# Normalised activations in tiles of 528 floats instead of 516

## The chip, the core and the metric

The kernel runs on one core of a Trainium2 chip. Its time is the device time of one execution, in microseconds (us). A profile is one execution recorded by the hardware profiler: which instruction ran on which engine, when, and what it waited for. The engines are TensorE (PE, with its weight loads shown apart as PEld), VectorE (DVE), ScalarE (ACT), GpSimd (POOL) and SyncE (SP); transfers run on 16 DMA engines. SBUF is the on-chip memory: 128 partitions, in each of which a tile takes the same bytes. "Alignment" in this text is the address of a tile within its partition, modulo 64.

## What is computed

One step of a two-layer backbone with 128 context and 128 latent tokens and a width of 2048. Per layer: a modulated RMSNorm, a mixer (attention and convolution in the first, a state-space model and grouped attention in the second), a modulated RMSNorm and an MLP with 8192 hidden features. Nearly all of the arithmetic is in the linears:

```python
for l in range(2):
    h = modulate(x, norm_g[l, 0], shift1, scale1)
    x = x + gate1 * mixer(h)                   # @ w_in, ..., @ w_out
    h = modulate(x, norm_g[l, 1], shift2, scale2)
    a = relu(h @ mlp_w1[l])
    x = x + gate2 * ((a * a) @ mlp_w2[l])
y = rms_norm(x, final_norm)
```

shift, scale and gate come from `silu(cond) @ ada_w[l] + bias`.

## The kernel before

Both token groups lie side by side as 256 columns, features on the partitions. A linear takes 128 outputs at a time: the weights come as pieces of 128x1024 floats (8 blocks of 128x128), by DMA into one of 8 `raw` tiles. Every float32 operand is split into a high half in a reduced format (F32R) and a low half, the rest. ScalarE casts the high half of a weight piece to `wh`, VectorE subtracts it to get `wl` (4 tiles each). Of activations the two halves lie in one tile: columns 0:256 high, 256:512 low. `block` (L453) then issues three matmuls for one block of weights and one tile of activations, all into the same PSUM tile `lin`: wh times high, wh times low, wl times high. `part` (L460) does so for the 8 blocks of a piece.

Tiles of activations come from two pools. The pool "hl" has 24 slots in rotation, of 516 floats each; it holds the normalised activations, the mixers' outputs and half or more of the MLP's hidden features. The pool "hid" holds the other hidden features in tiles of 512 floats: 8 in the first layer, 24 in the second. `put` (L543) fills a tile of either; both bear the name `hl` in the profile, so that hid tiles are told apart by the place in the program alone: in the w2 linears of `mlp` (L1685), tiles 0 to 7 of the 16 of a quarter of the hidden features are hid tiles and 8 to 15 hl tiles, but in the second quarter of the second layer all 16 are hid tiles. In `unnormed_tile` (L751) an hl tile holds 258 columns of each half (256 of the tokens and 2 of the shift), which is where 516 comes from; the first linears after a norm read them 258 wide, from columns 0:258 and 258:516.

A first pass, thrown away, keeps a clock for each engine and so finds the order in which the strands of the program take turns; the second builds the program in that order. Sizes of tiles in bytes play no part in it.

The pools lie one behind the other in SBUF: const (constants, among them `pk`, 866 floats loaded from one packed input, `ones`, `eps` and `pick2`), then x, "hl", raw, wh, wl, work, and the pools of a stage such as "hid". A tile's place is rounded up to 32 bytes. In the built program of before an hl tile takes 2064 bytes and 2080 of space, the first begins on a multiple of 64 bytes, and so do x, all raw, wh and wl tiles and all hid tiles. hl slots with an even number thus begin on a multiple of 64 bytes, those with an odd one 32 bytes past it. `eps` (L313) is the bias of the square root in `rstd_rows` (L659); `pick2` (L319) is a pair of 128x32 matrices with a one in column 0 or 1 and else zeros, with which `ada_vector` (L615) sums over the partitions on TensorE.

Of the kernel before, what the change touches and what calls it, by code (L numbers as in the profile page):

```python
# [19 lines left out]
EPS = 1e-6  # L20
# [28 lines left out]
class Engine:  # L49
    """An engine whose instructions are also charged to the program's clocks."""  # L50
# [27 lines left out]
class Line:  # L78
    """A strand of the program: a generator that says what its next instructions wait for."""
# [4 lines left out]
    def on_pe(self):  # L84
        """Whether its next instructions are for TensorE."""
        return callable(self.wait) and getattr(self.wait, "pe", False)
# [25 lines left out]
class Kern:  # L112
# [20 lines left out]
    # The program is many strands. A first run, that is thrown away, keeps a clock for each engine and always goes  # L133
    # on with a strand whose operands are there by then; the second run builds the program in that order, with
    # the weights loaded and split ahead of their use.
# [59 lines left out]
    def at(self, *aps):  # L195
        """When the tiles' contents are there."""
        return max([0] + [NEVER if v.tensor.name in self.held else self.at_.get(v.tensor.name, 0) for v in aps])

    def hold(self, t):
        """Not all of t is written yet."""  # L200
        self.held[t.tensor.name] = True
# [10 lines left out]
    def bulk(self, lead):  # L212
        """For work that is not urgent: the engines have come up to `lead` behind the clock of TensorE."""
        return lambda: max(self.clock["vector"], self.clock["scalar"]) + lead
# [58 lines left out]
    def get(self, *tags, on=None):  # L273
        """Waits for free slots (and for tiles), and takes them."""
        def ok():
            for t in set(tags):
                if self.live.get(t, 0) + tags.count(t) > self.cap[t]:
                    return False
            return self.when(on) + (MARGIN if "ps" in tags else 0)
        ok.pe = "ps" in tags  # L280
        yield ok
        for t in tags:
            self.live[t] = self.live.get(t, 0) + 1
# [10 lines left out]
    def setup(self):  # L294
        nc = self.nc
        self.const = self.pool("const", 1)
        self.xp = self.pool("xres", 1)
        self.hlp = self.pool("hl", 24)
        self.rawp = self.pool("raw", RAW)
        self.whp = self.pool("wh", SPLIT + 1)  # L300
        self.wlp = self.pool("wl", SPLIT + 1)
        self.work = self.pool("work", 2)
        self.ps = self.pool("ps", 1, PSUM)
        self.dram = self.pool("dram", 1, DRAM)
        pk = self.const.tile([128, _width(PACK)], F32, name="pk")
        nc.gpsimd.dma_start(pk, self.i["pack"])
        self.pk = {k: pk[:, a:b] for k, (a, b) in PACK.items()}
        self.x = self.xp.tile([128, KT, 256], F32, name="x")
        for q in range(2):
            nc.sync.dma_start(self.x[:, 8 * q:8 * q + 8], self.i["xT"][:, 8 * q:8 * q + 8])  # L310
        self.ones = self.const.tile([128, 128], F32, name="ones")
        nc.vector.memset(self.ones, 1.0)
        self.eps = self.const.tile([128, 1], F32, name="eps")  # L313
        nc.vector.memset(self.eps, EPS)
        self.ident = self.pk["ident"]
        self.condp = self.const.tile([128, KT, 32], F32, name="condp")
        nc.vector.memset(self.condp, 0.0)
        nc.scalar.activation(self.condp[:, :, 0:2], self.pk["cond"].rearrange("p (k c) -> p k c", c=2), AF.Silu)
        self.pick2 = self.const.tile([128, 2, 32], F32, name="pick2")  # L319
        nc.vector.memset(self.pick2, 0.0)  # L320
        for c in range(2):
            nc.vector.memset(self.pick2[:, c, c:c + 1], 1.0)
        self.mod, self.A, self.set_up = {}, {}, True
# [6 lines left out]
    def source(self, spec):  # L330
        """The columns of a piece, side by side."""
# [38 lines left out]
    def pump(self, upto=0):  # L370
        """Loads ahead, as far as there is room, and splits what has come (and the pieces before `upto` in any
        case)."""
# [24 lines left out]
    def slot(self, key, bufs, back=0):  # L397
        """When the slot of the next tile (or one after it) is free."""
# [4 lines left out]
    def peek(self, n, split=False):  # L403
        """When the next n raw tiles are there."""
# [5 lines left out]
    def take(self, split, *spec):  # L410
        """The next piece that has been loaded: its halves, or itself."""
# [32 lines left out]
    def there(self, X, a, b, weights=True):  # L444
        """For a wait: the tiles X[a:b], and the weights that come next."""
# [14 lines left out]
    def part(self, ps, src, X, a, b, first, last, w=None, **kw):  # L460
        """ps (+)= weight blocks a to b of a tile times X[a:b]."""
# [20 lines left out]
    def staged(self, srcs, X, width, groups, done, release=None):  # L482
        """Linears in groups: first all on the half of X that is there first."""
        n = 0
        for g in groups:
            # the first weights come before the banks are free
# [15 lines left out]
    def pairs(self, srcs, X, tags, done, cuts, between=None):  # L502
        """Linears side by side, two to a bank (of the given tags): first all on the part of X that is there first.
        done(n, ps, release) takes the tiles; between() is issued after the first part."""
# [16 lines left out]
        for i, (a, b) in enumerate(cuts):  # L521
            last = i == len(cuts) - 1
            # at the end one of each bank first: its copy out holds the bank
            for n in list(range(0, len(out), 2)) + list(range(1, len(out), 2)) if last else range(len(out)):
                ps, r = out[n]
                # the start of the first tile of a bank clears all of it
# [6 lines left out]
    def out_proj(self, src, X, done, held, between=None):  # L533
        """The tiles of an output projection, whose second half of X is there first."""
# [8 lines left out]
    def put(self, X, k, src, pool=None, slot=False):  # L543
        """X[k] = the halves of src."""
# [4 lines left out]
        t = (pool or self.hlp).tile([128, 512 if pool else 516], F32R, name="hl", tag="hl")  # L549
# [7 lines left out]
    def copied(self, dst, ps, note=None, release=None):  # L557
        """dst = ps, a linear's tile."""
# [10 lines left out]
    def ada(self, *pieces):  # L569
        """Two pieces (l, i, a, b) of the modulation: blocks a to b of vector i."""  # L570
# [44 lines left out]
    def ada_vector(self, n, pool):  # L615
        """Pieces of the modulation on VectorE, when it has time; TensorE only sums over the partitions."""
        nc = self.nc
        self.vnext = 0.0
        for piece in [(l, i, a, a + 8) for l, i in VECTOR[n] for a in (0, 8)]:
# [14 lines left out]
            for c in range(2):  # L634
                for b in range(4):
                    nc.tensor.matmul(ps[32 * b:32 * b + 32, 0:256], self.pick2[:, c], acc[:, c, 256 * b:256 * b + 256],
# [4 lines left out]
    def background(self):  # L641
        """The modulation in the order of its use: first parts of shift and scale, then theirs second."""
# [7 lines left out]
    def cuts(self, l, j):  # L650
        """The parts in which a modulated norm comes."""
        return FIRST if (l, j) == (0, 0) else ((0, 8), (8, 16))

    def mods(self, *keys):
        """For a wait: pieces of the modulation."""
        return lambda: self.at(*[self.mod[k] for k in keys]) if all(k in self.mod for k in keys) else False

# [1 line left out]
    def rstd_rows(self, sums, n, width, tag):  # L659
        """rstd of the sums in sums[:, :n] (token on the partition)."""  # L660
# [12 lines left out]
    def rstd_bcast(self, acc, width):  # L673
        """acc [128, 256]: squares summed over tiles; the rstd of each token on all partitions."""
# [20 lines left out]
    def sq_start(self, *norm):  # L695
        """The next norm's sum begins, and what doesn't wait for it."""
# [25 lines left out]
    def scales(self, l, j, a, b):  # L722
        """The factor of the modulated norm, with its gain."""
# [18 lines left out]
    # The first linears of a modulated norm don't wait for the sum over all of x: W (rstd A x + B) is  # L742
    # rstd (W A x) + W B, and B comes along as two more columns.
# [7 lines left out]
    def unnormed_tile(self, k, A, B, U):  # L751
# [8 lines left out]
        t = self.hlp.tile([128, 516], F32R, name="hl", tag="hl")  # L760
# [8 lines left out]
    def enter(self, l, j, srcs, groups, done):  # L769
        """The modulated norm of x; done(n, v, release) takes the first linears."""  # L770
# [36 lines left out]
    def residual(self, k, ps, l, i, summed, release=None, final=False):  # L807
        """x += gate * ps; the squares of the new x go to the next norm's sum if it has begun."""
# [17 lines left out]
    def softmax_parts(self, ps_list, scales, pool, tag, ebufs=2):  # L826
        """exp of the scaled scores (each a [128, 384] bank: prompt | sample) and the sums, per part."""
# [24 lines left out]
    def rope(self, out, src, rot, cos, sin, n, pool, tag, **kw):  # L852
        """out = src * cos + rot * sin for [128, n, 128] views."""
# [116 lines left out]
    def conv(self, gates, cins, cv, csum, mp, m2, mix):  # L970
# [21 lines left out]
        # layer norm of the convolution, silu  # L992
# [45 lines left out]
    def norm_heads(self, heads, ssq, ats, sub, m2, mix, hds):  # L1038
        """rms norm of the heads."""
# [206 lines left out]
    def gqa_scales(self, g, qss, qn, rqs, m2):  # L1246
        """The scale of each token's scores: rstd of the query, over sqrt(dim)."""
# [62 lines left out]
    def cmul(self, out_r, out_i, ar, ai, br, bi, tmp, neg_i=False):  # L1310
        """out = a * b, complex; tmp gives two scratch views of out's shape."""
# [13 lines left out]
    def s5_powers(self, kk, q1, z):  # L1325
# [4 lines left out]
        with ExitStack() as st:  # L1330
# [16 lines left out]
            # reduced angle: th - 2 pi n, with the product split so that it is exact  # L1347
# [33 lines left out]
            # k = (abar - 1) / a  # L1381
# [16 lines left out]
            # orders of powers: q1 for the chunk's state (7 - s | s), z for its output (i | 8 - i)  # L1398
# [111 lines left out]
    def s5(self, uts, mp, m2, fin, yhl):  # L1510
        """Two halves of the channels; the second one's states are prepared while the first one's are scanned."""
# [6 lines left out]
    def s5_states(self, qh, uts, mp, m2, out):  # L1518
        nc = self.nc
        u4 = range(4 * qh, 4 * qh + 4)  # L1520
        # u by (position in the chunk, channel) on the partition
# [29 lines left out]
        # states that each chunk adds  # L1551
# [38 lines left out]
    def s5_outputs(self, qh, u2, hs, mp, m2, fin, yhl):  # L1590
        nc = self.nc
        tt = nc.gpsimd.tensor_tensor
        # recurrence over the chunks (the backward half runs from the last)
# [22 lines left out]
        # outputs  # L1616
# [155 lines left out]
    def fill(self, most, goal, parts):  # L1772
        """How far the modulation pieces may run (in steps), and how far they have to within that many parts."""
# [47 lines left out]
def _channels():  # L1821
    """Order of the S5 channels: tile (qh, g4), partition (q', n)."""
# [101 lines left out]
```

## Time and profile before

| | |
|---|---|
| times of three runs, us | 2418.14, 2422.73, 2423.43 |
| median, us | 2422.73 |
| span of the profiled execution, us | 2417.9 |
| busy: PE, PEld, DVE, ACT, POOL | 96%, 88%, 70%, 48%, 7% |
| granted TensorE clock | 90% or more in 37 of the 40 slices |
| mean traffic of the memory | 260 GB/s |

Busy time of an engine is the time in which it ran instructions; matmuls overlap each other, so the mean duration of one is longer than the interval at which they start, and intervals are read from counts in a window or from starts in the timeline. The chain of waits goes back from the last instruction to whatever released it, and so on. [...]

### The profile page before, as it was taken

How to read it: one execution, taken by the hardware profiler on the slowest of the kernel's cores; microseconds unless marked ns; L12 is line 12 of the kernel's file. 1: busy time of each engine (PE TensorE's matmuls, PEld its weight loads, DVE VectorE, ACT ScalarE, POOL GpSimd, SP SyncE). 2: the span in 40 equal slices, each digit the busy share in tenths (PEclk: the TensorE clock that was granted, in tenths of full speed). 3: DMA queues.
4: the chain of work that ended last, by engine and by line, in shares of the span. 5: the costliest groups of instructions: out<-in, count | busy, mean ns of one | idle time of the engine just before them, and what ended most of it. 6: DMA issues, size and time to landing. Idle time of an engine off the chain costs nothing.

```text
span 2417.9 us, 49512 instructions
## 1 busy us (share of the span) xinstructions
PE 2331.7 (96%) x20152; PEld 2134.6 (88%) x20152; DVE 1696.8 (70%) x2957; ACT 1154.1 (48%) x1894; POOL 173.5 (7%) x293
## 2 busy tenths in 40 slices
PE   6999999999999999999999978999999999999997
PEld 1788887888999999999999857799999999999997
DVE  1489985677889898887666434566998855555555
ACT  2364457465444434434455644555744333443453
POOL 0000000000111011101000236000000000000000
PEclk9999999999999999999999988999999999999998
DMA  9979987879678898879877877765587855555552
GB/s 384 339 261 325 320 312 255 293 269 317 204 265 301 300 316 299 311 263 333 281 231 249 295 281 265 270 226 181 187 295 268 273 192 193 182 191 190 184 186 94
DMA packets 179638, 627.64 MB, mean 260 GB/s; under 512 B 21377, under 2 KB 21393, under 8 KB 179153
## 3 DMA queue, kind: packets, MB, share of 16 engines
q1 hardware_dynamic: 169920, 595.67, 71.1%
q0 software_dynamic: 9488, 28.81, 3.9%
q8 instruction: 158, 2.59, 0.4%
q14 instruction: 72, 0.58, 0.1%
HBM read 602.17 MB, written 26.41 MB: 260 GB/s over the span
## 4 chain that ended last, share of the span: by engine, by line
PE 85%; DVE 3%; DMA 3%; ACT 3%; POOL 3%; issue 1%; DVEq 0%; SPq 0%; ACTq 0%; POOLq 0%
PE lin L60 76%; PE ada L60 5%; POOL rt L60 2%; DVE wl L60 1%; DMA raw<-in_ada_w 1%; POOL hs L60 1%; ACT wh L60 1%; PE m1T L60 1%; DMA raw<-m3d 1%; ACT hs L60 0%; PE ps L60 0%; DMA raw<-in_ew_in 0%; PE po L60 0%; ACT L60 0%; DMA raw<-in_w 0%
## 5 line engine op out<-in xcount | busy, mean ns | idle before, releaser
L60 PE MATMUL lin<-hl,wh 128*128 128x256 f32 (+1 forms) x11200 | 2009.6, 282 | 7.2 <-ACT wh L60 7.0
L60 PEld LDWEIGHTS lin<-hl,wh 128*128 128x128 f32 x11200 | 1715.2, 189 | 98.4 <-issue 57.4
L60 PE MATMUL lin<-hl,wl 128*128 128x256 f32 (+1 forms) x5600 | 1569.9, 280 | 12.1 <-DVE wl L60 12.1
L60 PEld LDWEIGHTS lin<-hl,wl 128*128 128x128 f32 x5600 | 1058.2, 189 | 14.9 <-DVE wl L60 14.9
L60 DVE TENSOR_TENSOR wl<-raw,wh 128x1024 fp32r<-128x1024 f32 (+1 forms) x716 | 857.2, 1206 | 278.5 <-ACT wh L60 276.8
L60 ACT CAST wh<-raw 128x1024 fp32r<-128x1024 f32 (+1 forms) x716 | 738.6, 1035 | 520.0 <-PE lin L60 273.7
L60 PE MATMUL ada<-raw,condp 128*32 128x512 f32 (+1 forms) x1408 | 186.0, 572 | 19.5 <-DMA raw<-in_ada_w 19.3
L60 DVE SCALAR_TENSOR_TENSOR x<-lin,mod,x 128x128 f32<-128x128 f32 x320 | 97.1, 345 | 102.8 <-PE lin L60 102.6
L60 DVE SCALAR_TENSOR_TENSOR va<-raw,condp,va 128x1024 f32<-128x1024 f32 x120 | 148.4, 1277 | 0.0
L60 ACT ACTIVATE ms<-lin 128x256 f32<-128x256 f32 x114 | 43.8, 384 | 155.6 <-PE lin L60 155.6
L60 ACT CAST hl<-mq 128x256 fp32r<-128x256 f32 x128 | 51.8, 406 | 96.2 <-DVE mq L60 96.2
L60 DVE SCALAR_TENSOR_TENSOR cv<-cin,pke,cv 128x256 f32<-128x256 f32 x232 | 96.5, 476 | 0.0
L60 PEld LDWEIGHTS ada<-raw,condp 128*32 128x32 f32 x1408 | 32.8, 109 | 72.0 <-DMA raw<-in_ada_w 30.5
L60 DVE SCALAR_TENSOR_TENSOR mq<-lin,ms 128x256 f32<-128x256 f32 x114 | 47.9, 420 | 61.5 <-ACT ms L60 61.3
L60 ACT ACTIVATE sq<-x 128x256 f32<-128x256 f32 x75 | 31.0, 417 | 119.1 <-DVE x L60 117.1
L60 DVE TENSOR_TENSOR hl<-mq,hl 128x256 fp32r<-128x256 f32 x128 | 53.6, 421 | 28.3 <-ACT hl L60 28.1
L60 POOL TENSOR_TENSOR x<-x,rb 128x512 f32<-128x512 f32 (+1 forms) x2 | 4.2, 2133 | 916.6 <-ACT rb L60 916.6
L60 DVE TENSOR_TENSOR acc<-acc,sq 128x256 f32<-128x256 f32 x75 | 31.8, 424 | 32.2 <-ACT sq L60 30.4
L60 DVE TENSOR_TENSOR hl<-h,hl 128x256 fp32r<-128x256 f32 (+1 forms) x112 | 45.4, 420 | 9.1 <-ACT hl L60 8.7
L60 ACT CAST hl<-h 128x256 fp32r<-128x256 f32 (+1 forms) x112 | 42.8, 402 | 12.2 <-DVE h L60 11.5
L60 POOL DMA_DIRECT2D m3d<-m x32 | 21.6, 678 | 348.3 <-DVE m L60 347.1
L60 DVE TENSOR_TENSOR w<-s5z,bc 128x576 f32<-128x576 f32 x64 | 45.5, 752 | 0.6
(281 smaller groups left out, 1167.4 us busy)
## 6 DMA issues: line engine op xcount, KB each, us to landing
raw<-in_w SPq DMA_DIRECT2D x512, 512.0 KB, 5.1
raw<-in_ada_w SPq DMA_DIRECT2D x352, 512.0 KB, 6.1
raw<-in_ew_in SPq DMA_DIRECT2D x68, 512.0 KB, 6.0
raw<-in_ow_in SPq DMA_DIRECT2D x40, 512.0 KB, 6.5
raw<-in_ada_w SPq DMA_DIRECT2D x64, 256.0 KB, 6.2
raw<-in_ew_out SPq DMA_DIRECT2D x32, 512.0 KB, 6.2
raw<-in_ow_out SPq DMA_DIRECT2D x32, 512.0 KB, 4.7
m3d<-m POOLq DMA_DIRECT2D x32, 256.0 KB, 6.3
```

The lines of the kernel that those rows point to most:

```text
L60: return f(out, *a, **kw)
```

## The change

The two places that take a tile from the pool "hl" ask for 528 floats (2112 bytes, 33 x 64) instead of 516. Nothing else reads or writes the tiles in another way: the halves are at the same columns, and the last 12 floats stay unused. The 24 tiles take 768 bytes more than before, and SBUF would be overfull by that; two constants make room. `eps` becomes a last column of `pk`, set before the load of the others. `pick2` becomes two views of `condp`, the tile of the conditioning, whose columns 2 to 31 of each group are zero: column 10 of it is set to one, and the views begin at it and one column ahead of it; what else they hold reaches rows of the sum that nothing reads.

In the built program the order of the instructions is the same on every engine, but for the constants on VectorE: one column of `pk` is set first, `eps` and `pick2` (three memsets) are gone, one memset of a column of `condp` is new. The constants take 288 bytes less. The first hl tile therefore begins 32 bytes past a multiple of 64, and the next ones follow 2112 bytes apart.

| begins, modulo 64 bytes | before | after |
|---|---|---|
| hl tiles | 0 and 32 in turn (2080 apart) | 32 (2112 apart) |
| hid tiles (2048 apart) | 0 | 32 |
| x, raw, wh, wl | 0 | 32 |

The comments and docstrings that it also drops are left out here.

```diff
@@ setup
-        pk = self.const.tile([128, _width(PACK)], F32, name="pk")
-        nc.gpsimd.dma_start(pk, self.i["pack"])
+        w = _width(PACK)
+        pk = self.const.tile([128, w + 1], F32, name="pk")
+        self.eps = pk[:, w:w + 1]
+        nc.vector.memset(self.eps, EPS)
+        nc.gpsimd.dma_start(pk[:, 0:w], self.i["pack"])
...
-        self.eps = self.const.tile([128, 1], F32, name="eps")
-        nc.vector.memset(self.eps, EPS)
...
-        self.pick2 = self.const.tile([128, 2, 32], F32, name="pick2")
-        nc.vector.memset(self.pick2, 0.0)
-        for c in range(2):
-            nc.vector.memset(self.pick2[:, c, c:c + 1], 1.0)
+        nc.vector.memset(self.condp[:, 0, 10:11], 1.0)
+        cf = self.condp.rearrange("p k c -> p (k c)")
+        self.pick2 = [cf[:, 10 - c:42 - c] for c in range(2)]
@@ put
-        t = (pool or self.hlp).tile([128, 512 if pool else 516], F32R, name="hl", tag="hl")
+        t = (pool or self.hlp).tile([128, 512 if pool else 528], F32R, name="hl", tag="hl")
@@ ada_vector
-                    nc.tensor.matmul(ps[32 * b:32 * b + 32, 0:256], self.pick2[:, c], acc[:, c, 256 * b:256 * b + 256],
+                    nc.tensor.matmul(ps[32 * b:32 * b + 32, 0:256], self.pick2[c], acc[:, c, 256 * b:256 * b + 256],
@@ unnormed_tile
-        t = self.hlp.tile([128, 516], F32R, name="hl", tag="hl")
+        t = self.hlp.tile([128, 528], F32R, name="hl", tag="hl")
```

## Rows read from the trace of the kernel before

**Rows 1.** The page: span, busy time by engine, and the chain by line.

```profile
span 2417.9 us, 49512 instructions
...
PE 2331.7 (96%) x20152; PEld 2134.6 (88%) x20152; DVE 1696.8 (70%) x2957; ACT 1154.1 (48%) x1894; POOL 173.5 (7%) x293
...
PE lin L60 76%; PE ada L60 5%; POOL rt L60 2%; DVE wl L60 1%; DMA raw<-in_ada_w 1%; POOL hs L60 1%; ACT wh L60 1%; PE m1T L60 1%; DMA raw<-m3d 1%; ACT hs L60 0%; PE ps L60 0%; DMA raw<-in_ew_in 0%; PE po L60 0%; ACT L60 0%; DMA raw<-in_w 0%
```

**Rows 2.** Chain of waits in order of time, last long piece: start us, us.

```profile
1922.75 479.01 PE lin L60 x4122
```

**Rows 3.** Waits of PE: total us, times, longest us.

```profile
PE lin L60 <- DVE wl L60: 12.1, 10, 6.6
...
PE lin L60 <- ACT wh L60: 7.0, 3, 4.6
```

**Rows 4.** The page's groups: count | busy us, mean ns | idle before; by shape the 258-wide.

```profile
L60 PE MATMUL lin<-hl,wh 128*128 128x256 f32 (+1 forms) x11200 | 2009.6, 282 | 7.2 <-ACT wh L60 7.0
...
L60 PE MATMUL lin<-hl,wl 128*128 128x256 f32 (+1 forms) x5600 | 1569.9, 280 | 12.1 <-DVE wl L60 12.1
...
L60 PE MATMUL lin<-hl,wh 128*128 128x258 f32 x608 | 112.3, 286 | 0.0
```

**Rows 5.** Instructions on tile lin by window, columns in the first line.

```profile
core 0: us, PE busy (x) PEld busy (x) DVE busy (x) ACT busy (x), PEclk, DMA share, GB/s
1960.00:2040.00 80.00, 80.00 (x708) 80.00 (x707) 9.14 (x30) 0.00 (x0) 1.00 0.58 193
2050.00:2130.00 80.00, 80.00 (x680) 80.00 (x679) 5.95 (x14) 5.38 (x14) 1.00 0.56 188
515.20:526.40 11.20, 11.20 (x95) 11.20 (x94) 0.97 (x4) 0.00 (x0) 1.00 0.92 336
```

**Rows 6.** Timeline of PE where hid tiles end and hl begin: start us, us.

```profile
622.74 0.39 PE L60 MATMUL lin<-hl,wh 128*128 128x256 f32 x2
622.96 0.28 PE L60 MATMUL lin<-hl,wl 128*128 128x256 f32 x1
623.08 0.40 PE L60 MATMUL lin<-hl,wh 128*128 128x256 f32 x2
623.31 0.28 PE L60 MATMUL lin<-hl,wl 128*128 128x256 f32 x1
623.43 0.40 PE L60 MATMUL lin<-hl,wh 128*128 128x256 f32 x2
623.67 0.28 PE L60 MATMUL lin<-hl,wl 128*128 128x256 f32 x1
623.79 0.40 PE L60 MATMUL lin<-hl,wh 128*128 128x256 f32 x2
...
624.15 0.40 PE L60 MATMUL lin<-hl,wh 128*128 128x256 f32 x2
...
625.92 0.39 PE L60 MATMUL lin<-hl,wh 128*128 128x256 f32 x2
```

**Rows 7.** Timeline of PE over seven hid tiles at 865 us.

```profile
865.12 0.40 PE L60 MATMUL lin<-hl,wh 128*128 128x256 f32 x2
...
867.60 0.41 PE L60 MATMUL lin<-hl,wh 128*128 128x256 f32 x2
```

**Rows 8.** Groups by shape: writing the hl tiles.

```profile
L60 ACT CAST hl<-mq 128x256 fp32r<-128x256 f32 x128 | 51.8, 406 | 96.2 <-DVE mq L60 96.2
...
L60 DVE TENSOR_TENSOR hl<-mq,hl 128x256 fp32r<-128x256 f32 x128 | 53.6, 421 | 28.3 <-ACT hl L60 28.1 <-ACT ms L60 0.2
```

**Rows 9.** Timeline of the start on DVE, POOL and ACT.

```profile
0.95 0.06 DVE L60 MEMSET eps<- 128x1 f32 x1
...
1.52 0.25 DVE L60 MEMSET pick<- 128x64 f32 x3
...
1.28 0.71 POOL L60 DMA_DIRECT2D pk<-in_pack  x1 [0.83 <-POOLq L1916]
...
9.31 1.28 ACT L60 ACT_TABLE_LOAD   x1 [9.31 <-DMA pk<-in_pack]
```


## Prediction

> **What bounds the kernel now.** I read the page first: the profiled execution spans 2417.9 us and TensorE (PE) is busy for 96% of it [rows 1]. The chain of work that ended last says the same in another way: 76% of the span is PE on the linears, the instructions named `lin` [rows 1], and its last piece of any length, from 1922.75 us on, is 479.01 us of nothing but 4122 such matmuls in a row [rows 2]. What PE waits for ahead of them is small, 12.1 us for the low half of the weights and 7.0 us for the high half in the whole run [rows 3]. So the time is, nearly, a count of matmuls times the interval at which PE takes them. An edit of the placement of tiles can move the time by tens of microseconds in one way only: by changing that interval.
>
> The count: 11200 + 5600 = 16,800 `lin` matmuls [rows 4]. 608 of those on the high weights, and so half as many more on the low ones, 912 together, are 258 columns wide [rows 4]; the rest have 256. By the code (`mlp`), the w2 linears read 4 x 8 tiles of pool "hid" in the first layer and 40 in the second, each in 16 outputs with three matmuls: 72 x 16 x 3 = 3456. What is left, 16,800 - 912 - 3456 = 12,432, are 256-wide matmuls on tiles of pool "hl", the ones that the change makes longer.
>
> The interval: the three windows [rows 5] lie in stretches where PE never stops and the granted clock is 1.00. From 1960 to 2040 us PE reads hid tiles only: 708 matmuls touch the window, two or three of them over its edges, so 80 / 705.5 = 113.4 ns each. From 2050 to 2130 us it reads hl tiles only: 80 / 677.5 = 118.1 ns. The same instruction on the same weights' pools is 4.7 ns slower on an hl tile. 258-wide ones take 11.2 / 93 = 120.4 ns. The timeline shows one change from hid to hl within a linear [rows 6]: the last hid tile takes 0.34 us for its three matmuls (622.74 to 623.08), the eight hl tiles behind it 0.355 each (623.08 to 625.92). It is this difference, 12,432 x 4.7 ns = 58 us, that the change can win at most.
>
> **The change part by part.** *The long tiles.* Work, order and waits are the same, instruction by instruction. Before, hl tiles are 2064 bytes, laid out 2080 apart from a base on a multiple of 64: tiles at an even slot begin on a multiple of 64, those at an odd one 32 past it. hid tiles, 2048 apart, all begin on a multiple of 64, and so do the weights. If the start within 64 bytes were the cause, the even hl tiles would already run at hid's pace. They don't: the tiles from 623.08 on lie in slots 8, 1, 2, 3, ..., 7, and the first, third and fifth of them, on multiples of 64, are no faster than the second and fourth (0.35, 0.36, 0.36 us between the first four starts), and the very first hl tile, aligned and directly behind a hid tile, is slower at once, 0.35 us [rows 6]. Also the hid tiles, all aligned, can be slow: from 865.12 to 867.60, behind matmuls of the modulation, seven hid tiles took 2.48 us, 118.1 ns a matmul [rows 7]. I take from these rows that the start modulo 64 by itself is worth nothing, and cost the edit at 0.
>
> [...]
>
> *Where the tiles really lie.* The constants pool in front shrinks by 288 bytes (the 32-byte place of `eps` and the 256 of `pick2`), which is no multiple of 64. The hl base moves with it: all 24 tiles, now 2112 apart, begin 32 bytes past a multiple of 64, and so does everything behind them: x, raw weights, both halves of the split weights, hid. The change makes all hl tiles alike, but not aligned. Relative to the weights (modulo 64) they are now all as hid is; absolutely they are all as the odd slots were. No row of before shows an activation and a weight both at 32. The bounds: at best every hl matmul takes hid's 113.4 (-58 us); at worst hid loses its own pace and all take what the 258-wide ones take, whose second half is on no multiple of 32: 12,432 x 2.3 + 3456 x 7.0 = 53 us more. My value is 0, since odd hl tiles stand at 32 now and their cost is the same as that of the even ones.
>
> *Copies and casts.* ScalarE writes the high half of an hl tile in 406 ns and VectorE the low half in 421 ns [rows 8], on both kinds of slot; they are off the path, since PE waits 19.1 us in all for weights and nothing for these [rows 3]. 0. Loads of raw weights land 32 bytes off; PE's waits of 12.1 and 7.0 us are all that a dearer landing or cast would add to first. 0, and a few us for the range.
>
> *Setup.* The memsets of `eps` and `pick2` go, one of a column of `pk` (ahead of its load) and one of a column of `condp` come. The old ones lie between 0.95 and 1.77 us; ScalarE's first work waits for the load of `pk` until 9.31 us [rows 9]. That load was issued at 1.28 us, and the new 128x1 memset in front of it takes about 0.06 like that of `eps`. 0, and 0.1 us if its cover were gone. The `ada_vector` matmuls that read a view of `condp` in place of `pick2` are the same shape. 0.
>
> The sum is 0: the profiled execution (2417.9 us, at the low end of the runs shown) would repeat itself, and the median of 2422.7 as well. I forecast 2422 us.
>
> **The rivals.** *B, all relations become right: 2364 us.* If what matters is that the activation and the weight it meets lie alike modulo 64, as hid's do, every hl matmul falls to 113.4 ns: -58 us. For it: hid has this property at every tile, hl at every second only, and a slow tile could drag its neighbours, so that even and odd look alike. Against: the first hl tile behind hid has it and is slow [rows 6], and hid is slow at times [rows 7].
>
> *C, only the step to the next tile counts: about 2403 us.* hid steps by 2048 bytes, hl by 2080 before and 2112 after, now a multiple of 64. If one matmul in three, the first on a new tile, pays for the step, the gain is 12,432 / 3 x 4.7 = 19.5 us. For it: the hid tiles' step is the one thing that is always a multiple of 64. Against: inside a tile, the two matmuls on the high weights take 0.22 us on hid (622.74 to 622.96) and 0.23 to 0.24 on hl (623.08 to 623.31, 623.43 to 623.67), so the lateness is not all at the step [rows 6].
>
> *D, the other side, the change doesn't do what it says: about 2438 us.* All tiles, hid and weights with them, leave the multiples of 64. If hid is fast because it and its weights start there, its 3456 matmuls go to hl's pace: 3456 x 4.7 = 16 us more, and up to the 53 us above (2475) if hl suffers too. For it: hid is the only pool all on multiples of 64 and the only fast one. Against: aligned hl tiles are slow. It decides from the point where the lost pace of hid outweighs whatever hl gains, 1.3 ns a matmul.
>
> **How the numbers follow.** Chances: A (nothing) 0.36, B 0.18, C 0.17, D 0.29. A's own range is 2412 to 2432: the runs' 2418 to 2423, and half a nanosecond either way on 12,432 matmuls, as the pattern of slow and fast tiles shifts. The range for 8 in 10 reaches from B's 2364, less 2 us, to D's 2438 and some way towards its far end: 2362 to 2450; half of B and a quarter of D stay outside, 0.16 in all. A measurement of this kernel can tell about 0.2%, 5 us. Faster by more: B, C and a tenth of A, 0.39. Slower: D and a tenth of A, 0.33. Within: the rest of A, 0.28.
>
> **What would show it.** In windows of the last 479 us: hl at 118 and hid at 113.4 again is A; hl at 113.4 too is B, at 116.5 C; hid at 118 is D. The order and the number of matmuls must be the same, and PE's waits for weights stay near 19 us. If intervals of hl fall below 113 ns, or PE begins to wait for raw weights, I have the mechanism wrong altogether.

## The result, and the profile after

The changed kernel is slower: a median of 2438.19 us (2437.57 to 2448.36) against 2423.08 us for the kernel before on the same chip, a ratio of 1.0075 with a 95% interval from 1.0056 to 1.0094. Its profiled execution spans 2436.5 us, 18.6 more than that of before. The page, to be read against [rows 1, 4]:

```profile
span 2436.5 us, 49510 instructions
...
PE 2353.2 (97%) x20152; PEld 2156.7 (89%) x20152; DVE 1699.1 (70%) x2955; ACT 1153.8 (47%) x1894; POOL 173.3 (7%) x293
...
L60 PE MATMUL lin<-hl,wh 128*128 128x256 f32 (+1 forms) x11200 | 2032.0, 284 | 7.4 <-ACT wh L60 7.2
...
L60 PE MATMUL lin<-hl,wl 128*128 128x256 f32 (+1 forms) x5600 | 1574.8, 281 | 11.5 <-DVE wl L60 11.5
```

TensorE (PE) is busy 21.5 us longer with the same 20,152 matmuls; the other engines' busy time and PE's waits for weights (7.2 and 11.5 us) are as before. The last long piece of the chain of waits holds the same 4122 matmuls as in [rows 2] and is 8.77 us longer, with no wait in it:

```profile
1932.57 487.78 PE lin L60 x4122
```

So the same matmuls got slower. The windows, with the columns of [rows 5] (the first on hid tiles only, the second on hl tiles only):

```profile
1968.00:2048.00 80.00, 80.00 (x682) 80.00 (x681) 8.54 (x28) 0.00 (x0) 1.00 0.55 185
2058.00:2138.00 80.00, 80.00 (x677) 80.00 (x676) 5.95 (x14) 5.38 (x14) 1.00 0.56 189
```

With 2.5 matmuls off for the edges, hid takes 80 / 679.5 = 117.7 ns where it took 113.4, and hl 80 / 674.5 = 118.6 where it took 118.1. Over the whole trace, from the starts of neighbouring matmuls less than 160 ns apart (those in a row, with no wait between), the means are: hid 113.9 before and 117.8 after, 256-wide hl 117.9 and 118.6, 258-wide 120.4 and 120.6. All such intervals together are 1905.4 us before and 1928.5 after, 23.1 us more: 13.4 on hid, 9.3 on 256-wide hl, 0.4 on 258-wide. Everything else in the span is 4.5 us less, which leaves the 18.6 us. The places that the prediction costed at nothing are at nothing:

```profile
9.30 1.28 ACT L60 ACT_TABLE_LOAD   x1 [9.30 <-DMA pk<-in_pack]
```

ScalarE's first work waits for the load of `pk` as long as in [rows 9], and the casts to hl tiles take the 406 and 421 ns of [rows 8].

### The profile page after: what moved, and what is told of

It is laid out like the page before. It is cut to its first block, busy times and chain, and to the rows that moved or that the text cites. A ratio compares the mean times of both kernels' runs of the same rounds, so it can differ in the third digit from the quotient of the medians.

```text
span 2436.5 us, 49510 instructions
## 1 busy us (share of the span) xinstructions
PE 2353.2 (97%) x20152; PEld 2156.7 (89%) x20152; DVE 1699.1 (70%) x2955; ACT 1153.8 (47%) x1894; POOL 173.3 (7%) x293
## 4 chain that ended last, share of the span: by engine, by line
PE 86%; DMA 4%; ACT 3%; DVE 3%; POOL 3%; issue 1%; DVEq 0%; ACTq 0%; POOLq 0%; SPq 0%
PE lin L60 76%; PE ada L60 5%; POOL rt L60 2%; DMA raw<-in_ada_w 1%; DVE wl L60 1%; POOL hs L60 1%; ACT wh L60 1%; PE m1T L60 1%; DMA raw<-m3d 1%; ACT hs L60 0%; PE ps L60 0%; DMA raw<-in_w 0%; PE po L60 0%; DMA raw<-in_ew_in 0%; PE sc L60 0%
## 5 line engine op out<-in xcount | busy, mean ns | idle before, releaser
L60 PE MATMUL lin<-hl,wh 128*128 128x256 f32 (+1 forms) x11200 | 2032.0, 284 | 7.4 <-ACT wh L60 7.2
L60 PE MATMUL lin<-hl,wl 128*128 128x256 f32 (+1 forms) x5600 | 1574.8, 281 | 11.5 <-DVE wl L60 11.5
```

The lines of the kernel that those rows point to most:

```text
L60: return f(out, *a, **kw)
```

## Experiments

Two things had to be told apart. The loss has the size of rival D, which put it on the start of the tiles modulo 64 (theory S below). But the trace of before had already shown hid tiles on multiples of 64 at 118.1 ns [rows 7]. In what follows, "distance" is the address of an activation tile less that of the weights it meets, modulo 256 where nothing else is said. It is 64 for hid before; the hl tiles of before have all eight multiples of 32 in turn.

**All tiles back on multiples of 64 (a1_base64).** To the changed kernel, 32 bytes more among the constants, so that all that lies behind them moves up by 32:

```diff
         self.ident = self.pk["ident"]
+        self.const.tile([128, 8], F32, name="pad")
```

> Tiles of 528 floats as in the change, and 32 bytes of padding behind the constants, so that x, all hl, raw, wh, wl and hid tiles begin on a multiple of 64. Theory S (what counts is the start of the activation tile modulo 64, and a slow tile drags its neighbours): hid back to 113.4 to 114 ns a matmul, hl tiles fall from 118.6 to the same, time near 2365 us. Theory P (hid is fast for its step of 2048 bytes, and needs the start as well): hid back to 114, hl stays at 117 to 118.6, time 2415 to 2425 us. Theory W (the start of the weights counts): the same as P for hid, hl back to 117.9 as before, 2423 us.

Measured: 2441.35 us, ratio 1.0083 (1.0070 to 1.0096). hid 117.8 ns, hl 118.6, as without the padding. Windows on hid and on hl:

```profile
1972.00:2052.00 80.00, 80.00 (x681) 80.00 (x680) 8.54 (x28) 0.00 (x0) 1.00 0.58 186
2062.00:2142.00 80.00, 80.00 (x677) 80.00 (x676) 5.95 (x14) 5.38 (x14) 1.00 0.58 187
```

Every tile here does begin on a multiple of 64, the change's own aim, and nothing is won. S falls, and so do P and W for hid.

**The smaller constants alone (a2_consts516).** The other half of the change: everything moved by 288 bytes, hl tiles of 516 floats.

```diff
-        t = (pool or self.hlp).tile([128, 512 if pool else 528], F32R, name="hl", tag="hl")
+        t = (pool or self.hlp).tile([128, 512 if pool else 516], F32R, name="hl", tag="hl")
...
-        t = self.hlp.tile([128, 528], F32R, name="hl", tag="hl")
+        t = self.hlp.tile([128, 516], F32R, name="hl", tag="hl")
```

> The smaller constants of the change with the old tiles of 516 floats: hl tiles lie at 32 and 0 in turn, all else 32 past a multiple of 64. If the moved base is what costs: hid at 117.5 to 118 ns, hl within half a nanosecond of its 117.9, time about 2423 + 14 = 2437 us. If the longer tiles cost: hid at 114, time 2423 us.

Measured: 2422.52 us, ratio 1.0005 (0.9995 to 1.0014); hid 113.9 ns and hl 117.9, as before to a tenth. Window on hid:

```profile
1960.00:2040.00 80.00, 80.00 (x709) 80.00 (x708) 8.69 (x29) 0.00 (x0) 1.00 0.58 193
```

All tiles and weights but the odd hl slots' stand 32 past a multiple of 64, as in the changed kernel, and it costs nothing: moving everything together by 288 bytes changes nothing. It is the longer tile, that is the step of 2112 bytes instead of 2080, that costs the time, and it costs hid most, whose tiles it doesn't touch.

**hid alone, and the weights alone, moved by 32 bytes (a3_hid32, a4_w32).** To the kernel before, padding in front of one pool (for the weights also behind, so that the pools after them stay on multiples of 64):

```diff
+            self.pool("padh", 1, stack=st).tile([128, 8], F32, name="padh")
             hp = self.pool("hid", 8 + 16 * l, stack=st)
```

```diff
+        self.pool("pad0", 1).tile([128, 8], F32, name="pad0")
         self.whp = self.pool("wh", SPLIT + 1)
         self.wlp = self.pool("wl", SPLIT + 1)
+        self.pool("pad1", 1).tile([128, 8], F32, name="pad1")
```

> The kernel before with 32 bytes of padding in front of the pool hid alone: its tiles begin 32 past a multiple of 64, all else is in its old place. S: hid at 117.5 to 118 ns, hl 117.9 as before, about 2437 us. W: hid stays at 114, 2423 us. A theory by which the relation of activation and weight counts gives S's time too.

> The kernel before with 32 bytes of padding in front of the split weights wh and wl and 32 more behind them: only these tiles begin 32 past a multiple of 64, hid stays on multiples. S: hid stays at 114, 2423 us. W or the relation: hid at 118, about 2437 us.

Measured: 2441.81 us (1.0082, 1.0068 to 1.0096) and 2442.63 us (1.0083, 1.0068 to 1.0099). hid takes 119.8 ns in both, in the second although it stays on multiples of 64: with 64 bytes of padding in front of it and 32 in front of the weights its distance grows by 32 there, to 96, as in the first. Not the start but the distance counts here. This is called theory R below: the distance modulo 256 sets the interval. Window on hid of the first:

```profile
1970.00:2050.00 80.00, 80.00 (x669) 80.00 (x669) 8.54 (x28) 0.00 (x0) 1.00 0.56 183
```

**hid at other distances (b_hid64, b_hid128, b_hid192).** The same padding in front of hid with 64, 128 and 192 bytes.

> The kernel before with 64 bytes of padding in front of the pool hid alone: still on multiples of 64, now 128 past the weights modulo 256 instead of 64. S: hid stays at 113.9, 2421 us. R: hid takes another interval, by hl tiles at this distance in the changed kernel 119.6, about 20 us more, 2440 us.

> The same with 128 bytes: hid 192 past the weights modulo 256. S: 113.9, 2421 us. R: by hl tiles at this distance in the changed kernel 118.5, about 16 us more, 2436 us.

> The same with 192 bytes: hid at the same place as the weights modulo 256. S: 113.9, 2421 us. R: by hl tiles at this distance in the changed kernel 118.6, about 16 us more, 2437 us.

Measured in one run each: 2434.52, 2433.58 and 2444.02 us, with hid at 118.5, 117.3 and 119.8 ns and hl at 117.9 in all three. All three stand on multiples of 64, and none keeps 113.9. R was right that the distance decides, and off by 1 ns on each, since it took its figures from mixed hl tiles.

**hl tiles in hid's place (b1_hl512).** Distance 64 for all, by 64 bytes of padding in front of the pool "hl" and 192 behind it, which the cut of the edit leaves out:

```diff
-        t = (pool or self.hlp).tile([128, 512 if pool else 516], F32R, name="hl", tag="hl")
+        t = (pool or self.hlp).tile([128, 512], F32R, name="hl", tag="hl")
...
-        yield from self.staged(srcs, U, 258, groups, ...
+        yield from self.staged(srcs, U, 256, groups, ...
```

> The kernel before with hl tiles of 512 floats, 2048 bytes apart as hid's, and padding by which hl and hid tiles alike begin 64 past the weights modulo 256, as hid does before. The first linears after a norm are 256 wide instead of 258; the two columns of the shift are left out (ones take their place). Theory R (the distance from the weights to the activations modulo 256 sets the interval, with two levels that a stretch keeps once it is in one): all matmuls run at one of hid's two levels, mostly 113.4 ns and after gaps 117.8, so between 2360 us and 2420 us less some 2 us for the narrower ones. Theory S, the start modulo 64 with a drag: the same 2360 us. If the pool itself is slow for another reason (who writes it, what else runs then): hl stays at 117.9, near 2418 us.

Measured: 2428.94 us, ratio 1.0029 (1.0018 to 1.0040). Not one pace but two, 113.3 and 117.8 ns, for hl and hid alike, and mostly the slow one. Two windows, both across hid and hl tiles in turn:

```profile
1083.00:1091.00 8.00, 8.00 (x73) 8.00 (x73) 1.81 (x6) 0.00 (x0) 1.00 0.78 249
1104.00:1112.00 8.00, 8.00 (x71) 8.00 (x70) 1.21 (x4) 0.00 (x0) 1.00 1.01 367
```

From 1081.6 us, behind eight matmuls of the modulation, four parts of 24 run at 113.3 and hand it on from hl to hid and back; behind eight matmuls of another kind (`m1T`) the next are at 117.8, and hand that on:

```profile
1080.57 1.06 PE L60 MATMUL ada<-raw,condp 128*32 128x512 f32 x8
...
1092.56 1.04 PE L60 MATMUL m1T<-pk,m1t 128*128 128x128 f32 x8
```

PE does not idle there; other matmuls come in between. 29 of the kernel's 700 parts run at 113.3. So hl tiles are not slow of themselves, and at distance 64 there are two levels, which in these stretches last until other matmuls come between.

**TensorE alone (m1, m2).** The same three matmuls per block with nothing else running, in stretches of mostly 72, PE waiting some 0.5 us ahead of each (one run each; positions in floats, the loop condensed):

```python
for k in range(8):
    a, w = d + pitch * k, 128 * k
    out += [(w, a, 256), (w, a + 256, 256), (WL + w, a, 256)]   # weights, activations, columns
```

> Not the model but TensorE alone: three matmuls for each of 8 blocks as in the linears, on zeros, with the distance from weights to activations as the only thing that changes between stretches of 72 matmuls; the outputs are filled with zeros. Theory R: the interval of a stretch depends on the distance modulo 256: near 118 or 113.4 ns at 64, 119.8 at 96, 118.5 at 128, 117.8 or 114 at 192, 120 at 0, and the same again 256 and 512 bytes on, with no other engine at work. Theory S: 113.4 at every multiple of 64. If something else in the kernel (casts, loads) makes the difference: 113.4 or less at every distance. Some stretches begin with one matmul of another width, with tiles of another pitch, or with one tile at another distance: by the part of R that has two levels, these decide between 113.4 and 117.8 in the stretch behind, and a wait alone gives one of them or the other.

Timeline of m1: start, duration of a stretch; the first three rows are distances 0, 64 and 96, then 112 and, 256 bytes on, 320, 352 and 368:

```profile
75.64 8.89 PE L1971 MATMUL lin<-act,wt 128*128 128x256 f32 x72 [0.46 <-ACT s L1973]
...
112.82 8.75 PE L1971 MATMUL lin<-act,wt 128*128 128x256 f32 x72 [0.52 <-ACT s L1973]
...
131.40 8.89 PE L1971 MATMUL lin<-act,wt 128*128 128x256 f32 x72 [0.52 <-ACT s L1973]
140.80 8.48 PE L1971 MATMUL lin<-act,wt 128*128 128x256 f32 x72 [0.52 <-ACT s L1973]
...
261.78 8.75 PE L1971 MATMUL lin<-act,wt 128*128 128x256 f32 x72 [0.52 <-ACT s L1973]
...
280.36 8.89 PE L1971 MATMUL lin<-act,wt 128*128 128x256 f32 x72 [0.52 <-ACT s L1973]
289.77 8.48 PE L1971 MATMUL lin<-act,wt 128*128 128x256 f32 x72 [0.52 <-ACT s L1973]
...
1025.98 6.03 PE L1971 MATMUL lin<-act,wt 128*128 128x120 f32 x49 [0.52 <-ACT s L1973]
1032.53 5.82 PE L1971 MATMUL lin<-act,wt 128*128 128x128 f32 x49 [0.52 <-ACT s L1973]
```

From the starts of the last 24 matmuls of each stretch, ns a matmul:

| distance, bytes | 0 | 16 | 32 | 48 | 64 | 80 | 96 | 112 |
|---|---|---|---|---|---|---|---|---|
| interval | 120.0 | 116.6 | 117.8 | 118.3 | 117.8 | 118.4 | 120.0 | 113.3 |
| **distance** | **128** | **144** | **160** | **176** | **192** | **208** | **224** | **240** |
| interval | 118.5 | 118.4 | 117.3 | 119.2 | 117.8 | 118.9 | 118.2 | 117.0 |

The same series came back at 256, 512 and 768 bytes more, and at 1024 as far as it was measured, but for 16, which took 118.6 there. The kernel's own hid tiles agree with it within 0.5 ns at 64 (the slow level), 96, 128, 192 and 0. No cast, load or store is needed for any of this: in seven windows of m1 within such stretches ScalarE is busy 0.00 us on `lin` and the share of DMA is 0.00 or 0.01. At 64 with this step, a wait alone gave 117.8 every time; one matmul of another width ahead gave 113.3 for 5 of 24 widths (the last two rows: 120 columns first, 49 matmuls in 6.03 us, and 128 columns first, 5.82 us); eight tiles ahead at a step of 2080 or 2112 bytes gave it for one of eight first distances each. So what comes ahead decides the level here. One tile at another distance ahead gave it for one of eight, 32. Two of these stretches have the kernels' own sequences: eight tiles at distances 0, 32, ..., 224, as the hl tiles ahead of most hid tiles in the first layer of the kernel before, then sixteen at 64; and the same with 0, 64, 128, 192 twice, as in the changed kernel. The sixteen end at 113.3 in the first and at 117.8 in the second:

```profile
1239.11 8.52 PE L1971 MATMUL lin<-act,wt 128*128 128x256 f32 x72 [0.52 <-ACT s L1973]
...
1313.40 8.76 PE L1971 MATMUL lin<-act,wt 128*128 128x256 f32 x72 [0.52 <-ACT s L1973]
```

m1 also moved the low weights alone, with the high ones at 64: 117.7 to 117.8 at six of eight places, but 113.3 with the low weights 128 bytes further and 115.7 with 192. So their distance counts as well; in the kernels it is the same as that of the high weights.

> As m1, TensorE alone on zeros. If the distance modulo 256 from the weights to the activations decides and nothing else: tiles that step by 2080 bytes over weight blocks that step by 544 keep their distance and run at one interval like those of 2048 over 512 (113.3 ns at 112 bytes, 120 at 0); steps of 2080, 2112, 2176 over 512 mix the intervals of all distances and come out at 117 to 119 ns whatever the first distance. If the absolute address of the tiles or of the weights plays a part as well, 2080 over 544 is no better than 2080 over 512. At a distance of 112 bytes the stretches behind another width or other tiles stay at 113.3 if there is only one level at this distance; if there are two, some go to 117.8.

In m2, steps of 2080 or 2112 bytes gave 118.3 to 119.0 ns whatever the first distance, a step of 2176 between 116.7 and 118.8, and a step of 2304, nine times 256, one pace for each first distance again: 120.0 at 0, 116.6 at 32, 113.3 at 64, 120.1 at 96, 120.0 at 128, 118.7 at 160, 113.3 at 192, 118.3 at 224. Of these eight only 0, 96 and 224 repeat the table; at 64 and at 192 it is 4.4 ns less. (In m1, eight tiles at a step of 2304, gone through three times over the same weights, took 117.8 at 64; in m2 there are 24 tiles over three pieces of weights.) Tiles stepping 2080 over weights stepping 544 keep their distance too and took 116.9 to 120.3, 119.0 at 112; 2112 over 576 took 116.1 to 118.4. So the distance modulo 256 alone does not set the pace: the table holds for tiles 2048 apart over blocks 512 apart, behind a wait. At 112, all 56 stretches, behind whatever widths or tiles, ended at 113.3: no second level showed with this step. Two rows at 112, behind tiles at a step of 2080 and of 2112, and two at a step of 2304 with first distances of 64 and 96:

```profile
481.72 8.59 PE L1966 MATMUL lin<-act,wt 128*128 128x256 f32 x72 [0.52 <-ACT s L1968]
...
554.53 8.60 PE L1966 MATMUL lin<-act,wt 128*128 128x256 f32 x72 [0.52 <-ACT s L1968]
...
1014.92 8.43 PE L1966 MATMUL lin<-act,wt 128*128 128x256 f32 x72 [0.52 <-ACT s L1968]
1023.87 8.90 PE L1966 MATMUL lin<-act,wt 128*128 128x256 f32 x72 [0.52 <-ACT s L1968]
```

The first two have eight tiles of mixed distances and the way back to 113.3 in their time, the third runs at 113.3 throughout, the last at 120.0.

**The changed kernel at other distances (c3_off12).**

```diff
         t = (pool or self.hlp).tile([128, 512 if pool else 528], F32R, name="hl", tag="hl")
+        if not pool:
+            t = t[:, 12:528]
```

> The changed kernel, nothing moved but the use of an hl tile: columns 12 to 527 of the 528 instead of 0 to 515. Its distances from the weights are then 48, 112, 176, 240 bytes modulo 256 instead of 0, 64, 128, 192. By the intervals of TensorE alone at these (118.3, 113.3, 119.2, 117.1: mean 117.0, against 120, 117.8, 118.5, 117.8: mean 118.5) hl falls by about 1.5 ns, 19 us. hid lies where it lies in the changed kernel: if its slow level there is handed on by the hl tiles ahead of it, some of its parts go to 113.3, up to 15 us more; if its own place is the cause, it stays at 117.8. So 2405 to 2420 us against 2438; if only steps count, 2438.

Measured: 2437.04 us, ratio 1.0069 (1.0056 to 1.0082). hl fell by 0.6 ns, to 118.0, not by 1.5, and hid stayed at 117.8. A mean of the bare intervals was a poor forecast here, where the distance changes at every tile, and this run did not show hid's level turned by the tiles ahead of it.

**One distance for all hl tiles (c1_576, its control c2_ctl, and c4_576wl3).** Tiles of 576 floats, used from column 4, with 96 bytes of padding in front of the pool and 160 behind: all at 112. The room comes from buffers; the padding and the tag of 4 are not in the cut:

```diff
-RAW = 8
+RAW = 7
...
-        t = (pool or self.hlp).tile([128, 512 if pool else 528], F32R, name="hl", tag="hl")
+        t = (pool or self.hlp).tile([128, 512 if pool else 576], F32R, name="hl", tag="hl")
+        if not pool:
+            t = t[:, 4:520]
```

> hl tiles 2304 bytes apart (576 floats, used from column 4), all 112 bytes past the weights modulo 256; hid stays at 64. To make room there are 7 raw tiles instead of 8 and a tag of the second mixer has 4 instead of 5. If the distance decides: hl at 113.4 throughout, 12,432 x 4.5 = 56 us less than before; hid at 113.4 if it takes over the fast level from hl, at 117.8 if not (15 us); so 2365 to 2385 us plus what the smaller buffers cost (its control). If activations in the kernel don't follow TensorE alone: hl at 117 to 118, 2420 us or more.

> The control: hl tiles of 516 floats as before, with 7 raw tiles and 4 of the tag. All distances as before, so hid at 113.9 and hl at 117.9; the time differs from 2421 us by the cost of the smaller buffers alone, 0 to 10 us.

Measured: c1_576 2420.84 us, ratio 1.0002 (0.9991 to 1.0014); its control 2449.05 us, 1.0124 (1.0109 to 1.0139). hl takes 114.1 ns in the one and 117.9 in the other. Against its control the distance gained 28 us, and the two smaller buffers cost 28, where 0 to 10 were expected. By the intervals alone the gain would have been 12,432 x 3.7 less 3456 x 3.1, some 35 us; where the rest went is not shown. hid is at 117.8 in the one and 114.6 in the other. Windows of c1_576 on hid and on hl, the reverse of [rows 5]:

```profile
1967.00:2047.00 80.00, 80.00 (x682) 80.00 (x681) 8.53 (x28) 0.00 (x0) 1.00 0.57 187
2057.00:2137.00 80.00, 80.00 (x708) 80.00 (x707) 5.94 (x14) 5.40 (x14) 1.00 0.60 194
```

c4_576wl3 has 8 raw tiles again and takes the room from the low weights:

```diff
-        self.wlp = self.pool("wl", SPLIT + 1)
+        self.wlp = self.pool("wl", SPLIT)
```

> As c1_576 (all hl tiles 112 bytes past the weights modulo 256, hid at 64), but with the 8 raw tiles back and 3 wl tiles instead of 4 for the room. If the distance is worth on the whole kernel what its intervals say, 12,432 x 3.8 = 47 us less for hl and 13 us more for hid, and the third wl tile's loss costs less than the eighth raw tile's (28 us), the time is between 2387 and 2415 us, faster than both kernels; if the wl tile costs as much, 2421 us.

Measured: 2392.64 us (2390.28 to 2395.44), ratio 0.9887 (0.9870 to 0.9903): 28.7 us faster than the kernel before on the same chip, and faster than the changed one. hl 114.1 ns, hid 117.8. By the intervals the gain would be 47 - 13 = 34 us, which leaves some 5 for the lost wl tile and the tag of 4 together; so the 28 above were mostly the raw tile. Page, last long piece of the chain, and the window on hl:

```profile
span 2388.5 us, 49668 instructions
```

```profile
1897.65 474.66 PE lin L60 x4122
```

```profile
2022.00:2102.00 80.00, 80.00 (x708) 80.00 (x708) 5.84 (x14) 5.40 (x14) 1.00 0.58 192
```

The 4122 matmuls of the last piece take 474.66 us, against 479.01 before [rows 2] and 487.78 after the change.

## Why the prediction was wrong

**What bounds the kernel: right.** The time is the count of matmuls times their interval; the interval moved, and with it the time.

**The long tiles, costed at 0: wrong, and this is the step that failed.** The rows had shown that the start modulo 64 explains nothing (even and odd hl slots alike, aligned hid slow at times), and a2_consts516 bears that out. But from "this variable does not matter" I concluded "placement does not matter", while the same rows showed hid and hl 4.7 ns apart, and left that difference without a cause. What the runs showed in its place: the pace depends on where activations and weights lie to each other, modulo 256 rather than 64 (a2 against a3 and a4, then m1), and on the tiles that come ahead, which hand on a level. The change turns the hl tiles' eight distances into four (0, 64, 128, 192): hl got 0.7 ns dearer, 9 us, and hid lost its fast level, 3.9 ns on 3456 matmuls, 13 us. The hl loss is not that of dropping the cheaper distances: at the four that stay, hl took 118.5, 117.3, 118.2 and 117.4 ns before and 118.6, 117.8, 119.6 and 118.5 after, so the tiles around one count too. My bounds modulo 64 were the wrong ones; that the time stayed within them was luck.

**D gave the number, not the reason.** It said 2438 us with hid at 118, and both came. Its mechanism, hid leaving the multiples of 64, is refuted from both sides: leaving them costs nothing (hid at 113.9 ns in a2_consts516), and returning gains nothing (117.8 in a1_base64). What was right in D is that hid's pace can be lost by an edit of other tiles.

**B and C were nearer to the mechanism.** B named the relation of activation and weight, C the step from tile to tile; both used 64 where the runs show 256. With that number, a step of 2112 has no advantage over 2080 (64 and 32 modulo 256; 118.3 to 119.0 ns for both in m2), and 2304 keeps one distance; which first distance is then worth its room only a measurement told (113.3 to 120.1 in m2). B's bound of 113.4 ns on hl is what c4_576wl3 nearly reaches (114.1).

**Setup, copies, loads: right**, at 0 within the trace.

**Why hid lost its level.** Its own distance is the same 64 in before, a2_consts516, a1_base64 and the changed kernel; what differs is the hl tiles ahead of it. With the addresses of the program laid beside the trace, 98 parts of 24 hid matmuls in the kernel before follow hl tiles without a gap. The 91 behind tiles whose last distances are 128, 160, 192, 224 take 113.3 ns; the 7 that end at 32 or 96, each in the first w2 linear of a quarter, take 117.8. The starts of one part of each kind and of what follows it, 24 matmuls later:

```profile
609.12 0.40 PE L60 MATMUL lin<-hl,wh 128*128 128x256 f32 x2
...
611.95 0.41 PE L60 MATMUL lin<-hl,wh 128*128 128x256 f32 x2
...
614.80 0.39 PE L60 MATMUL lin<-hl,wh 128*128 128x256 f32 x2
...
617.51 0.40 PE L60 MATMUL lin<-hl,wh 128*128 128x256 f32 x2
```

That is 2.83 us behind tiles that end at 32, and 2.71 behind tiles that end at 224. In the changed kernel all 98 of these parts follow tiles of its four distances, and all take 117.8. m1 gives the same two outcomes for TensorE alone (its rows at 1239.11 and 1313.40), so it is the hl tiles ahead that turn hid's level.

Open: which property of the tiles ahead selects the level. The last four do not settle it: in c2_ctl, 23 of 45 parts behind 128, 160, 192, 224 take 117.8, where of the eight tiles ahead one differs (0 for 32). Whether the weights that count are those in use or those being loaded at the same time (PEld is busy for 80.00 us of the windows of 80, as PE is), no run separates. What in the chip makes the period of 256 bytes and the two levels, no run here shows.

## What to carry to other kernels

Where matmuls of one kind run at two paces with nothing else different, don't test the alignment of one operand: move everything together, then each operand alone; if the first does nothing (here hid stayed at 113.9 ns) and the second does (119.8 with hid or the weights moved by 32 bytes), the distance between them counts. Look also at what runs just ahead: the tiles that lost most here were not moved against their weights at all. Here a step of 2304, a multiple of 256, paid at one first distance (112); look for such a distance in a bare measurement, with the kernel's own steps, before paying for it. And price the room: 28 us gained by placement were lost in one kernel mostly to a load buffer, and kept in another by taking a different buffer.

## What the runs showed of the hardware

- With tiles 2048 bytes apart over weight blocks 512 apart, behind a wait and at a granted clock of 1.00, the interval of a 256-column matmul with its own weight load depends on the distance between activations and weights modulo 256: 113.3 ns at 112 bytes, 116.6 to 120.0 at the other multiples of 16 (m1). With other steps the same distance can give another pace: 119.0 at 112 (2080 over 544), 113.3 at 64 and 192 (2304 over 512, m2).
- A common shift does nothing: by 288 bytes hid stays at 113.9 ns (a2_consts516), by 32 at 117.8 (a1_base64 against the changed kernel). hid alone moved by 32 takes 119.8 where it took 113.9 (a3_hid32). Every move here is by a multiple of 16 bytes; what a smaller one does is not shown.
- At 64 bytes there are two levels, 113.3 and 117.8 ns. The fast one lasted through 768 matmuls in a row in the kernel before; eight matmuls of another kind ended it in b1_hl512. Tiles ahead at other distances can lead into either (m1, and hid in the kernel before).
- Which of PE's matmuls gets slower says little on which tiles were moved: the hl tiles grew, and 13 of the 23 us were lost on hid.
